# A two-model stack of ten phases: paired 512-column products and a hand-written order under the last blocks of each contraction

## The chip, the cores and the metric

The kernel runs on one core of a Trainium2 chip, as one launch. The metric is the device time of that core in microseconds, the median of several runs. The times before are 2337.38, 2338.28 and 2340.46 us (median 2338.28).

## The reference, cut to what matters

Two transformer stacks run one after the other on 256 tokens of width 1024 (`x`), the first with 256 context tokens (`ctx`) beside them. All tensors are fp32.

```python
def half_ffn(h, m, k, g_pre, g_post, w_in, w_out):          # first stack, D_FF = 2816
    y = swiglu(modulated_norm(h, g_pre, m, k), w_in, w_out)
    return gated_residual(h, y, g_post, m, k, 0.5)
# layer 0: half_ffn (x and ctx), differential attention, half_ffn (x and ctx)
# layer 1: half_ffn (x and ctx), grouped attention (x alone onward), half_ffn (x)
def gated_residual(h, y, g, m, k, weight):
    return h + weight * m[..., k + 2, :] * rmsnorm(y, g)
# second stack, one layer
x = x + 0.5 * swiglu_2(rmsnorm_2(x, norm_ffn1), ffn1_gate, ffn1_up, ffn1_down)
x = x + merged(dilated attention, block attention, two gates) @ w_out
x = x + 0.5 * swiglu_2(rmsnorm_2(x, norm_ffn2), ffn2_gate, ffn2_up, ffn2_down)
return rmsnorm_2(x, norm_final)
```

So there are nine contractions back to width 1024 (six SwiGLU, two attention outputs, the mixer's output), and each is followed by a residual, a norm over the row, and the next phase's products.

## The kernel before, in words

**Numbers.** Every fp32 operand is split into a high part (rounded to fp32r) and a low part (the rest). A product is three matmuls into one PSUM tile (`mm3`, L126 to L130): high by high (L128), weights high by low or low by high (L129), and the third cross term (L130). A weight is loaded by DMA into `raw`, split by ScalarE (high, L118) and VectorE (low, L119) into `wh`, `wl` (or into arena units `u`).

**Phases.** `run` goes through ten phases: three SwiGLU phases on 512 tokens (`T == 512`), differential attention (512 tokens, after the first of them), grouped attention, three SwiGLU phases on 256 tokens (`T == S`), the hybrid mixer (256 tokens, before the last of these), and a final norm. Within a SwiGLU phase the features go by pairs of 128-blocks: `half(q, c, t0, t1)` (L668) multiplies one 128-block of the gate (`q = 0`) or up (`q = 1`) weights with the input over 8 blocks of 128 rows; that is 24 matmuls of 256 columns on 256 tokens and 24 of 512 columns on 512 tokens. `post` (L677) takes SiLU of the gate PSUM tile, multiplies with the up tile and splits the result. On 256 tokens the first two of the eleven pairs are done token by token (`lead_tokens`, L624), the other nine by `half`. In the mixer, `project` (L1310) does 8 blocks by `columns` (L552), also 24 matmuls of 256 columns. In differential attention, six of the eight heads are projected in between the attention steps: `first` does the first 256 tokens of a block, `second` the other 256.

**The end of a contraction (an edge).** `contract` (L414) runs over the rows of the down weight. The last 4 or 6 row blocks (the tail) go token tile by token tile, so that tile 0 is done first, then its residual and norm can run while the PE works on tile 1. `gated` (L358) is the residual of the first stack: `products` multiplies with the gate row (VectorE, L368) and then squares the same half for the norm (ScalarE, L340); `stat` takes the root on GpSimd (L346); `add` adds into `h` (L378). `stats` (L486) of the next phase squares `h` (L340), takes the root, scales the rows (L502); `turn` (L506) transposes them on the PE (L514) and applies scale and bias: ScalarE into a scratch tile (L523), VectorE copy to the high part (L524) and difference to the low (L525), or without bias L123 and L124. Then the first products of the next phase (its leads) can start. `Order` collects all these steps with due times worked out from the length of the pieces and calls them in that order. The framework's scheduler then orders the emitted instructions of each engine by its own model, so that the due times set priorities and not the final order.

**Queues.** SyncE issues nearly all DMAs; `raw` has 5 buffers, `wh`/`wl` share 8, scratch tiles have 6, PSUM 8 banks. ScalarE, VectorE and GpSimd each run their instructions in the order in which they stand.

## Time and profile before

| | before |
|---|---|
| median of 3 runs | 2338.28 us |
| the profiled execution | 2339.77 us |
| its span (first to last instruction) | 2338.0 us |
| PE busy | 2277.9 us, 97% |
| DVE busy | 1471.0 us, 63% |
| ACT busy | 1016.7 us, 43% |
| matmuls | 13275 |

PE is the matmul engine, DVE is VectorE, ACT is ScalarE, POOL is GpSimd. The ends of matmuls in the trace are modelled and overlap, so a matmul's cost is read from start to start (its pitch), and a short PE stall shows as a longer pitch, not as idle time. Nine edges stand in the trace; eight lie at 380, 680, 1040, 1418, 1532, 1724, 1920 and 2120 us (30 us each), the ninth at the end. They are called edges 1 to 9 below. Edges 1 to 4 lead into phases on 512 tokens, edges 5 to 8 into phases on 256; from edge 6 on the rows of the next phase need no bias. A view by windows gives, for each stretch, its length, then the busy time of PE, PEld (weight loads), DVE, ACT and POOL with the count of instructions, the granted PE clock, the DMA share and GB/s.

### The profile page before, as it was taken

Reading aid. Unit: us, or ns where it says so; the run is one execution under the profiler, and the core shown is the slowest. Engines: PE = TensorE matmul, PEld = TensorE weight load, DVE = VectorE, ACT = ScalarE, POOL = GpSimd, SP = SyncE. Lnnn points to the kernel's source line nnn. Section 1 sums busy time; section 2 is a strip of 40 time slices with the busy share of each in tenths; the row PEclk is TensorE's granted clock in tenths of the full one; section 3 lists DMA queues with packets and bytes.
Section 4 is the critical chain, followed back from the end, with each engine's and each line's share of the span. In section 5 each row is a group of like instructions: output and inputs, shape, how many; then the busy total and the mean of one; then the engine's idle time right before and its main releaser. Section 6 shows DMA issues by size and latency. Waiting matters only on the chain.

```text
span 2338.0 us, 33744 instructions
## 1 busy us (share of the span) xinstructions
PE 2277.9 (97%) x13275; PEld 1984.2 (85%) x13275; DVE 1471.0 (63%) x2334; ACT 1016.7 (43%) x1831; POOL 84.7 (4%) x130
## 2 busy tenths in 40 slices
PE   7999999998899999999999999999999999999998
PEld 5888887888788788888888887789989989999997
DVE  4866474578767753746866626775555557877554
ACT  4322223566653232134322225765445546655543
POOL 0000000111100000000000001100000002000000
PEclk9999999999999999999999999999999999999999
DMA  9655364321225643652665542145665575546664
GB/s 283 210 186 180 117 228 133 100 64 38 90 72 163 181 146 106 218 160 73 203 185 170 168 139 78 55 154 181 191 197 162 181 235 169 144 129 198 172 181 143
DMA packets 270951, 361.46 MB, mean 155 GB/s; under 512 B 11472, under 2 KB 222280, under 8 KB 270792
## 3 DMA queue, kind: packets, MB, share of 16 engines
q1 hardware_dynamic: 270464, 359.17, 49.5%
q8 instruction: 104, 1.70, 0.3%
q14 instruction: 55, 0.45, 0.1%
q10 hardware_dynamic: 328, 0.14, 0.0%
HBM read 355.02 MB, written 4.24 MB: 154 GB/s over the span
## 4 chain that ended last, share of the span: by engine, by line
PE 60%; DVE 5%; ACT 3%; issue 1%; DMA 1%; POOL 1%; POOLq 0%; DVEq 0%; ACTq 0%
PE ps L128 19%; PE ps L129 19%; PE ps L130 19%; DVE u L119 1%; DVE wl L119 1%; ACT junk L340 1%; DVE u L378 1%; ACT u L118 0%; DVE s_l L525 0%; ACT wh L118 0%; PE ps L514 0%; POOL sm L346 0%; DVE scr L368 0%; PE ps L257 0%; DMA raw<-in_ffn_up_dram 0%
## 5 line engine op out<-in xcount | busy, mean ns | idle before, releaser
L128 PE MATMUL ps<-s_h,wh 128*128 128x256 f32 (+1 forms) x2560 | 835.3, 327 | 5.5 <-ACT u L1019 3.6
L129 PE MATMUL ps<-s_l,wh 128*128 128x256 f32 (+1 forms) x2560 | 831.7, 325 | 0.6 <-DVE s_l L525 0.5
L130 PE MATMUL ps<-s_h,wl 128*128 128x256 f32 (+1 forms) x2560 | 830.2, 324 | 0.2 <-DVE wl L119 0.2
L119 DVE TENSOR_TENSOR wl<-raw,wh 128x1024 fp32r<-128x1024 f32 x458 | 550.3, 1210 | 422.3 <-ACT wh L118 420.6
L118 ACT ACTIVATE wh<-raw 128x1024 fp32r<-128x1024 f32 x458 | 475.1, 1047 | 572.8 <-PE ps L129 509.9
L128 PEld LDWEIGHTS ps<-s_h,wh 128*128 128x128 f32 x2560 | 486.6, 190 | 52.0 <-ACT u L1019 4.2
L129 PEld LDWEIGHTS ps<-s_l,wh 128*128 128x128 f32 x2560 | 486.8, 190 | 41.7 <-DVE s_l L525 2.3
L130 PEld LDWEIGHTS ps<-s_h,wl 128*128 128x128 f32 x2560 | 486.7, 190 | 39.4 <-DVE wl L119 0.4
L128 PE MATMUL ps<-wh,s_h 128*128 128x512 f32 (+1 forms) x976 | 367.0, 376 | 0.4 <-DVE s_h L524 0.4
L129 PE MATMUL ps<-wl,s_h 128*128 128x512 f32 (+1 forms) x976 | 363.8, 373 | 0.0
L130 PE MATMUL ps<-wh,s_l 128*128 128x512 f32 (+1 forms) x976 | 363.5, 373 | 0.0
L244 DVE SCALAR_TENSOR_TENSOR u<-raw,sc,u 128x1024 f32<-128x1024 f32 x224 | 277.1, 1279 | 80.3 <-DMA raw<-in_ada_w_dram 80.1
L128 PEld LDWEIGHTS ps<-wh,s_h 128*128 128x128 f32 x976 | 184.5, 189 | 33.0 <-DVE s_h L524 0.6
L130 PEld LDWEIGHTS ps<-wh,s_l 128*128 128x128 f32 x976 | 184.2, 189 | 32.2
L129 PEld LDWEIGHTS ps<-wl,s_h 128*128 128x128 f32 x976 | 184.4, 189 | 31.1
L118 ACT ACTIVATE s_h<-scr 128x256 fp32r<-128x256 f32 (+1 forms) x144 | 74.1, 514 | 304.2 <-DVE scr L682 287.1
L129 PE MATMUL ps<-u,s_h 128*128 128x512 f32 (+1 forms) x312 | 117.2, 376 | 1.3 <-DVE u L119 1.3
L128 PE MATMUL ps<-u,s_h 128*128 128x512 f32 (+1 forms) x312 | 117.8, 378 | 0.0
L130 PE MATMUL ps<-u,s_l 128*128 128x512 f32 (+1 forms) x312 | 116.9, 375 | 0.0
L682 DVE TENSOR_TENSOR scr<-scr,ps 128x512 f32<-128x512 f32 (+1 forms) x120 | 67.6, 564 | 77.6 <-PE ps L130 75.9
L680 ACT ACTIVATE scr<-ps 128x512 f32<-128x512 f32 (+1 forms) x120 | 58.8, 493 | 106.2 <-PE ps L130 99.5
L346 POOL TENSOR_TENSOR sm<-sm,mhalf 128x1 f32<-128x1 f32 x50 | 27.5, 553 | 1993.8 <-DVE sm L345 1993.8
(183 smaller groups left out, 1941.0 us busy)
## 6 DMA issues: line engine op xcount, KB each, us to landing
raw<-in_ffn_w_in_dram SPq DMA_DIRECT2D x176, 512.0 KB, 4.1
raw<-in_ada_w_dram SPq DMA_DIRECT2D x144, 512.0 KB, 4.6
raw<-in_ffn_w_out_dram SPq DMA_DIRECT2D x88, 512.0 KB, 4.1
raw<-in_ffn_gate_dram SPq DMA_DIRECT2D x44, 512.0 KB, 5.3
raw<-in_ffn_up_dram SPq DMA_DIRECT2D x44, 512.0 KB, 5.0
raw<-in_ffn_down_dram SPq DMA_DIRECT2D x44, 512.0 KB, 4.3
raw<-in_w_in_dram SPq DMA_DIRECT2D x44, 512.0 KB, 4.8
raw<-in_da_w_in_dram SPq DMA_DIRECT2D x24, 512.0 KB, 3.8
```

Source lines behind the costliest of these rows:

```text
L118: self.nc.scalar.activation(hi, src, AF.Copy)
L119: self.nc.vector.tensor_tensor(lo, src, hi.bitcast(F32), ALU.subtract)
L128: mm(out, lhi, rhi, start=start, stop=False)
L129: mm(out, lhi, rlo, start=False, stop=False)
L130: mm(out, llo, rhi, start=False, stop=stop)
L244: nc.vector.scalar_tensor_tensor(acc[s][h], raw, x, acc[s][h], ALU.mult, ALU.add)
L340: self.nc.scalar.activation(self.junk, src, AF.Square, scale=1.0 / 32, accum_out=ss)
L346: nc.gpsimd.tensor_tensor(r, v, self.mhalf, ALU.pow)
L378: nc.vector.scalar_tensor_tensor(h[:, sl], st.yg[k], st.r, h[:, sl], ALU.mult, ALU.add)
L680: self.nc.scalar.activation(sg, pg[:, 0:T], AF.Silu)
L682: self.nc.vector.tensor_tensor(hf, sg, pu[:, 0:T], ALU.mult)
```

## The change

1. **Paired parts.** A new class `Pair` keeps the high and the low part of one input block side by side in 512 columns. `mm_pair` multiplies the weights' high part with both at once (one matmul of 512 columns in place of two of 256), leaving the two sums in the two halves of the PSUM tile, and the weights' low part with the high part (256 columns). `halves` adds them: a ScalarE copy of the right half and a VectorE add of the left. It is used in `half` on 256 tokens and in the mixer's `project`. The low-part matmuls stand last but one.
2. **Row-block pieces.** In differential attention `first` and `second` each do 4 row blocks over all 512 columns, in place of 8 row blocks over 256 columns each.
3. **Gate first.** SiLU is taken right after the gate's product, ahead of the up product.
4. **Squares ahead.** In `gated` the squares of a half are a step of their own, ahead of the gate products of the same half, and `stat` comes ahead of the second products.
5. **Written order.** All that `Order` issues at an edge is put in a region in which every engine keeps the written order. The due times are new (a 512-column matmul 0.227 instead of 0.216), transposes of the first two tiles are spread by 1.8 us, those of the other two stand after all four leads, and the leads' weights are loaded from 0.5 or 1 us on after the tail's beginning.
6. **Bias.** In `turn`, every second block's high part is written by ScalarE straight from PSUM, not by a VectorE copy.

```diff
+class Pair:
+    def __init__(self, pool, name, nblk):
+        self.u = [pool.tile([P, 2, 512], F32R, tag="u", name=f"{name}_p{u}") for u in range(nblk // 2)]
+    def both(self, k):
+        return self.u[k // 2][:, k % 2, :]
+    def at(self, which, k, c0=0, c1=S):
+        return self.both(k)[:, S * which + c0:S * which + c1]
...
+    def mm_pair(self, out, w, x, n):
+        mm = self.nc.tensor.matmul
+        for b in range(n - 1):
+            mm(out, w(b)[0], x.both(b), start=b == 0, stop=False)
+        for b in range(n):
+            mm(out[:, 0:S], w(b)[1], x.at(0, b), start=False, stop=False)
+        mm(out, w(n - 1)[0], x.both(n - 1), start=False, stop=True)
...
+    def halves(self, p):
+        f = self.scr([P, S])
+        self.nc.scalar.activation(f, p[:, S:512], AF.Copy)
+        self.nc.vector.tensor_tensor(f, f, p[:, 0:S], ALU.add)
+        return f
...
-        def products(k):
+        def squares(k):
             if k == 0:
                 st.ss = self.small(2)
+            self.half_squares(y[k], st.ss[:, k:k + 1])
+        def products(k):
             t = self.scr([P, 512])
             nc.vector.tensor_tensor(t, y[k], g[:, k * 512:(k + 1) * 512], ALU.mult)
-            self.half_squares(y[k], st.ss[:, k:k + 1])
             st.yg.append(t)
...
-        return [(-half, lambda: products(0)), (0.0, lambda: products(1)), (1.6, stat), (2.6, add)], 3.61, 0.6
+        return [(1.6 - half, lambda: squares(0)), (3.3 - half, lambda: products(0)), (0.0, lambda: squares(1)),
+                (0.9, stat), (1.0, lambda: products(1)), (1.9, add)], 3.4, 0.7
...
-        step = 0.216 * 6 * tail
+        step = 0.227 * 6 * tail
...
-        o.issue()
+        with self.tc.manual_schedule():
+            o.issue()
...
-        return [(-half, lambda: squares(0)), (0.0, lambda: squares(1)), (1.0, rstd), (1.8, rows)], 1.85
+        return [(-half, lambda: squares(0)), (0.0, lambda: squares(1)), (0.9, rstd), (1.8, rows)], 2.8
...
+                if q % 2:
+                    modulate(hi)
+                else:
+                    nc.vector.tensor_copy(hi, f)
...
-        self.xT = self.k.asplit(KB, self.T)
+        self.xT = k.asplit(KB, self.T) if self.T == 512 else Pair(k.ar, k.nm("s"), KB)
...
-                    o.add(ready[2 * s + 1] + (1.76, 0.0)[s] + 0.33 * kk,
+                    o.add((ready[1] + 1.8 * kk, self.go + 8.8 + 0.01 * kk)[s],
...
-            o.add(t_end - 5.86 + q, lambda q=q: dma(q))
-            o.add(t_end - 5.66 + 4 * q, lambda q=q: split(q))
+            o.add(0.5 + q, lambda q=q: dma(q))
+            o.add(1.5 + 2.5 * q, lambda q=q: split(q))
...
+        if self.T == S:
+            self.k.mm_pair(p, w, self.xT, KB)
+            return
...
+    def gate_values(self, pg):
         k, T = self.k, self.T
+        x = k.halves(pg) if T == S else pg
+        sg = x if T == S else k.scr([P, T])
+        self.nc.scalar.activation(sg, x, AF.Silu)
+        return sg
+    def post(self, j, sg, pu):
+        k, T = self.k, self.T
+        if T == S:
+            pu = k.halves(pu)
...
-                    self.columns(r.p, r.w, 0, S)
+                    self.columns(r.p, r.w, 0, 512, range(4))
...
-                    self.columns(r.p, r.w, S, 512)
+                    self.columns(r.p, r.w, 0, 512, range(4, KB))
...
-        self.columns(p, self.k.wcols(self.w, c0), 0, S)
-        return p[:, 0:S]
+        k.mm_pair(p, lambda b: [x[:, b, :] for x in w], self.xT, KB)
+        return k.halves(p)
```

**Place A**, the PE in a SwiGLU phase on 256 tokens: `s..h` and `s..l` are input blocks (high, low), `wh` and `wl` weights, a name's number a buffer. Before, six matmuls of one half:

```order
L128 MATMUL ps2772_15697<-s2664_h0_15004,wh2767_15688 128x256
L129 MATMUL ps2772_15697<-s2664_l0_15005,wh2767_15688 128x256
L130 MATMUL ps2772_15697<-s2664_h0_15004,wl2768_15689 128x256
L128 MATMUL ps2772_15697<-s2664_h1_15006,wh2769_15692 128x256
L129 MATMUL ps2772_15697<-s2664_l1_15007,wh2769_15692 128x256
L130 MATMUL ps2772_15697<-s2664_h1_15006,wl2770_15693 128x256
```

Now a whole half, 16 matmuls:

```order
L151 MATMUL ps2449_13317<-s2332_p0_12674,wh2445_13309 128x512 x2
L151 MATMUL ps2449_13317<-s2332_p1_12675,wh2445_13309 128x512 x2
L151 MATMUL ps2449_13317<-s2332_p2_12676,wh2447_13313 128x512 x2
L151 MATMUL ps2449_13317<-s2332_p3_12677,wh2447_13313 128x512
L153 MATMUL ps2449_13317<-s2332_p0_12674,wl2446_13310 128x256 x2
L153 MATMUL ps2449_13317<-s2332_p1_12675,wl2446_13310 128x256 x2
L153 MATMUL ps2449_13317<-s2332_p2_12676,wl2448_13314 128x256 x2
L153 MATMUL ps2449_13317<-s2332_p3_12677,wl2448_13314 128x256 x2
L154 MATMUL ps2449_13317<-s2332_p3_12677,wh2447_13313 128x512
```

The L128 and L129 of a block have become one row of 512 columns, and the low weights come after seven of the eight wide ones.

**Place B**, ScalarE at edge 6: `wh`, `u` from `raw` are weight splits of the next phase's leads, `junk` from `ps` the squares of the contraction's halves (`ps2600`, `ps2601` tile 0), `junk` from `u` the squares of the next norm, `s` from `ps` the transposed rows. Before:

```order
L118 ACTIVATE u2679_15054<-raw2677_15044 128x1024
L340 ACTIVATE junk_80,sm2683_15068<-ps2600_14688 128x512
L118 ACTIVATE u2681_15058<-raw2678_15046 128x1024
L340 ACTIVATE junk_80,sm2683_15068<-ps2601_14689 128x512
L340 ACTIVATE junk_80,sm2688_15111<-u1147_6110 128x512 x2
L340 ACTIVATE junk_80,sm2689_15120<-ps2602_14702 128x512
L123 ACTIVATE s2664_h0_15004<-ps2694_15137,n2c_595 128x128 x3
L123 ACTIVATE s2664_h1_15006<-ps2695_15156,n2c_595 128x128
```

Now (`ps2618`, `ps2619` are tile 0):

```order
L132 ACTIVATE u2697_14585<-raw2695_14581 128x1024
L132 ACTIVATE u2699_14589<-raw2696_14583 128x1024
L371 ACTIVATE junk_80,sm2701_14605<-ps2618_14217 128x512
L371 ACTIVATE junk_80,sm2701_14605<-ps2619_14218 128x512
L371 ACTIVATE junk_80,sm2706_14642<-u1147_5825 128x512 x2
L371 ACTIVATE junk_80,sm2710_14664<-ps2620_14231 128x512
L137 ACTIVATE s2682_p0_14533<-ps2711_14666,n2c_595 128x128 x2
L137 ACTIVATE s2682_p1_14534<-ps2711_14666,n2c_595 128x128 x2
L137 ACTIVATE s2682_p2_14535<-ps2712_14685,n2c_595 128x128 x2
```

Both lead splits now stand ahead of both squares, and the transposed blocks of one PSUM tile are done in a row, not mixed with the other's.

**Place C**, VectorE at the same edge: L368 is now L402 (gate products), L345 is L376 (sum for the root), L378 is L411 (add). Before:

```order
L368 TENSOR_TENSOR scr2684_15069<-ps2600_14688,u2593_14674 128x512
L119 TENSOR_TENSOR u2680_15055<-raw2677_15044,u2679_15054 128x1024
L119 TENSOR_TENSOR u2682_15059<-raw2678_15046,u2681_15058 128x1024
L368 TENSOR_TENSOR scr2685_15090<-ps2601_14689,u2593_14674 128x512
L345 SCALAR_TENSOR_TENSOR sm2686_15099<-sm2683_15068 128x1
```

Now:

```order
L133 TENSOR_TENSOR u2698_14586<-raw2695_14581,u2697_14585 128x1024
L133 TENSOR_TENSOR u2700_14590<-raw2696_14583,u2699_14589 128x1024
L402 TENSOR_TENSOR scr2702_14613<-ps2618_14217,u2611_14203 128x512
L376 SCALAR_TENSOR_TENSOR sm2703_14622<-sm2701_14605 128x1
L402 TENSOR_TENSOR scr2705_14626<-ps2619_14218,u2611_14203 128x512
```

The second products have gone behind the sum for the root, and no weight split stands between the two halves of tile 0. On the PE at edge 1 the first eight transposes stood after 84 of the tail's 96 matmuls; now the first four stand after 78, four more after 90, and the other eight at the end.

## Rows read from the trace of the kernel before

**Rows 1.** The page: busy us, share of the span and instructions per engine.

```profile
PE 2277.9 (97%) x13275; PEld 1984.2 (85%) x13275; DVE 1471.0 (63%) x2334; ACT 1016.7 (43%) x1831; POOL 84.7 (4%) x130
```

**Rows 2.** Timeline, 256-column matmuls (start us, us, engine, line, operation, out<-in).

```profile
1800.10 0.28 PE L128 MATMUL ps<-s_h,wh 128*128 128x256 f32 x1
...
1804.78 0.28 PE L128 MATMUL ps<-s_h,wh 128*128 128x256 f32 x1
```

**Rows 3.** Timeline, 512-column matmuls.

```profile
299.84 0.39 PE L130 MATMUL ps<-wh,s_l 128*128 128x512 f32 x1
...
303.92 0.39 PE L130 MATMUL ps<-wh,s_l 128*128 128x512 f32 x1
```

**Rows 4.** Timeline, 128x256 operations like those that halves adds.

```profile
1800.84 0.36 ACT L680 ACTIVATE scr<-ps 128x256 f32<-128x256 f32 x1
...
1802.82 0.42 DVE L682 TENSOR_TENSOR scr<-scr,ps 128x256 f32<-128x256 f32 x1 [0.63 <-PE ps L130]
```

**Rows 5.** Windows of three stages and of the half-clock stretches.

```profile
480.00:660.00 180.00, 163.34 (x1138) 148.14 (x1138) 139.65 (x406) 113.90 (x304) 27.83 (x40) 0.96 0.17 57
619.00:626.00 7.00, 5.61 (x23) 4.91 (x24) 5.52 (x20) 4.41 (x13) 0.73 (x1) 0.52 0.84 285
640.00:646.00 6.00, 6.00 (x22) 5.24 (x23) 4.00 (x17) 2.56 (x9) 0.69 (x1) 0.50 0.00 0
1742.00:1746.00 4.00, 4.00 (x17) 3.32 (x16) 1.70 (x5) 1.22 (x4) 0.00 (x0) 0.57 0.00 0
1760.00:1920.00 160.00, 160.00 (x1159) 152.19 (x1158) 89.23 (x104) 79.41 (x104) 0.00 (x0) 1.00 0.63 195
1945.00:2010.00 65.00, 62.48 (x505) 60.98 (x504) 53.30 (x111) 49.05 (x110) 8.01 (x9) 1.00 0.56 159
```

**Rows 6.** Windows of edges 1 to 8, 30 us each: the sum.

```profile
sum 240.00, PE 228.15 PEld 194.26 DVE 156.70 ACT 130.61 POOL 32.85; mean PE 28.52 PEld 24.28 DVE 19.59 ACT 16.33 POOL 4.11
```

**Rows 7.** Timeline of the PE at edge 6: tail's first matmul, then the transposes.

```profile
1724.80 0.39 PE L128 MATMUL ps<-u,s_h 128*128 128x512 f32 x1
...
1739.53 0.39 PE L130 MATMUL ps<-u,s_l 128*128 128x512 f32 x1
1741.78 0.74 PE L514 MATMUL ps<-ident,u 128*128 128x128 f32 x4 [1.86 <-DVE u L502]
```

**Rows 8.** Timeline of ACT at edge 6: lead split, squares, transposed blocks.

```profile
1731.16 1.06 ACT L118 ACTIVATE u<-raw 128x1024 fp32r<-128x1024 f32 x1 [0.27 <-DMA raw<-in_ffn_gate_dram]
...
1733.38 1.05 ACT L118 ACTIVATE u<-raw 128x1024 fp32r<-128x1024 f32 x1
1736.38 0.60 ACT L340 ACTIVATE junk<-ps 128x512 bf16<-128x512 f32 x1 [1.96 <-DVE scr L368]
...
1742.55 0.37 ACT L123 ACTIVATE s_h<-ps,n2c 128x128 fp32r<-128x128 f32 x1 [0.66 <-PE ps L514]
1743.33 0.37 ACT L123 ACTIVATE s_h<-ps,n2c 128x128 fp32r<-128x128 f32 x1 [0.42 <-DVE s_l L124]
```

**Rows 9.** Timeline of DVE at edge 6: lead split, products, rows.

```profile
1735.61 0.68 DVE L368 TENSOR_TENSOR scr<-ps,u 128x512 f32<-128x512 f32 x1
...
1741.23 0.88 DVE L502 TENSOR_SCALAR u<-u,sm 128x512 f32<-128x512 f32 x2
```

**Rows 10.** Timeline of ACT at edge 1: tile 1's norm squares, first scaled blocks.

```profile
398.07 0.63 ACT L340 ACTIVATE junk<-u 128x512 bf16<-128x512 f32 x1
...
401.53 1.93 ACT L523 ACTIVATE scr<-ps,mods,amod 128x256 f32<-128x256 f32 x4 [1.26 <-PE ps L514]
```

**Rows 11.** Timeline of the PE at edge 1: tail's first matmul, transposes, first lead.

```profile
380.31 0.39 PE L128 MATMUL ps<-u,s_h 128*128 128x512 f32 x1
...
400.95 0.98 PE L514 MATMUL ps<-ident,u 128*128 128x128 f32 x7 [1.32 <-DVE u L502]
...
406.83 0.28 PE L128 MATMUL ps<-s_h,wh 128*128 128x256 f32 x1
...
409.43 0.28 PE L128 MATMUL ps<-s_h,wh 128*128 128x256 f32 x1
```

More of the change, by code (lines that the diff above doesn't have):

```diff
@@ L522, in turn @@
                 f = k.scr([P, w])
-                nc.scalar.activation(f, pt[:, q, :], AF.Identity, scale=A[:, b:b + 1], bias=B[:, b:b + 1])
-                nc.vector.tensor_copy(hi, f)
+                modulate = lambda to: nc.scalar.activation(to, pt[:, q, :], AF.Identity,
+                                                           scale=A[:, b:b + 1], bias=B[:, b:b + 1])
+                modulate(f)
+                if q % 2:
+                    modulate(hi)
+                else:
+                    nc.vector.tensor_copy(hi, f)
                 nc.vector.tensor_tensor(lo, f, hi.bitcast(F32), ALU.subtract)
     def enter(self, o, done, t_end):
-        self.xT = self.k.asplit(KB, self.T)
+        k = self.k
+        self.xT = k.asplit(KB, self.T) if self.T == 512 else Pair(k.ar, k.nm("s"), KB)
         self.xn = [None] * self.nt
@@ L534, in enter @@
             ready.append(done[t][0] + took)
-        self.go = max(t_end, ready[self.nt // 2 - 1] + (1.76 + 3 * 0.33 + 0.1 if self.T == 512 else 0.97 + .1))
+        self.go = max(t_end, ready[self.nt // 2 - 1] + (5.5 if self.T == 512 else 1.1))
         self.ready = ready
@@ L545, in enter @@
                 for kk in range(2):
-                    o.add(ready[t] + 0.97 * kk, lambda t=t, kk=kk: self.turn((t,), range(4 * kk, 4 * kk + 4)))
+                    o.add(ready[t] + 1.0 * kk, lambda t=t, kk=kk: self.turn((t,), range(4 * kk, 4 * kk + 4)))
         self.lead(o, t_end)
@@ L550, in lead, with columns @@
         pass
-    def columns(self, p, w, t0, t1):
+    def columns(self, p, w, t0, t1, blocks=range(KB)):
         hi, lo = w
-        for b in range(KB):
+        for b in blocks:
             self.k.mm3(p[:, t0:t1], hi[:, b, :], lo[:, b, :],
@@ L618, in lead @@
         for q in range(2):
-            o.add(t_end - 5.86 + q, lambda q=q: dma(q))
-            o.add(t_end - 5.66 + 4 * q, lambda q=q: split(q))
+            o.add(0.5 + q, lambda q=q: dma(q))
+            o.add(1.5 + 2.5 * q, lambda q=q: split(q))
             for c in range(2):
-                o.add(self.go + 5.2 * q + 2.6 * c, lambda q=q, c=c: self.half(q, c, 0, S))
+                o.add(self.go + 5.8 * q + 2.9 * c, lambda q=q, c=c: self.half(q, c, 0, S))
     def lead_tokens(self, o, t_end):
@@ L670, in half @@
         p = self.p[q][c]
[L671 to L680 removed]
+        cc = slice(c * P, (c + 1) * P)
+        w = lambda b: [x[:, b % 4, cc] for x in self.w[q][b // 4]]
+        if self.T == S:
+            self.k.mm_pair(p, w, self.xT, KB)
+            return
+        for b in range(KB):
+            self.k.mm3(p[:, t0:t1], *w(b), self.xT.at(0, b, t0, t1), self.xT.at(1, b, t0, t1), b == 0, b == KB - 1)
+    def gate_values(self, pg):
+        k, T = self.k, self.T
+        x = k.halves(pg) if T == S else pg
[6 more added lines that the diff above has]
+            pu = k.halves(pu)
         hf = k.scr([P, T])
[L682 removed]
+        self.nc.vector.tensor_tensor(hf, sg, pu, ALU.mult)
         k.split(self.hT.at(0, j), self.hT.at(1, j), hf)
@@ L707, in body @@
             t0 = self.begun if jp == 0 else 0
+            pg = [None, None]
             for q in range(2):
@@ L716, in body @@
                         late.pop(0)()
-                    if q:
+                    if q == 0:
+                        pg[c] = self.gate_values(p[c])
+                    else:
                         self.post(2 * jp + c, pg[c], p[c])
-                pg = p
                 if jp + 1 < NJ // 2:
@@ L879, in lead @@
             self.started.append(r)
-            o.add(t_end - 8 + 2.6 * n, lambda r=r, h=h, part=part: self.block(part, h, r))
-            o.add(self.go + 2.6 * n, lambda r=r: self.columns(r.p, r.w, 0, S))
+            o.add(1 + 1.3 * n, lambda r=r, h=h, part=part: self.block(part, h, r))
+            o.add(self.go + 2.9 * n, lambda r=r: self.columns(r.p, r.w, 0, S))
     def setup(self, o, t_end):
@@ L1121, in load @@
                 self.wq[kp] = k.wpair(self.w, kp, 0)
-            o.add(t_end - 8 + 2.6 * kp, load)
-            o.add(self.go + 2.6 * kp, lambda kp=kp: piece(kp))
+            o.add(1 + 1.3 * kp, load)
+            o.add(self.go + 2.9 * kp, lambda kp=kp: piece(kp))
     def rope_tables(self, o, t_end):
@@ L1310, in project @@
     def project(self, c0):
-        p = self.k.ps()
-        self.columns(p, self.k.wcols(self.w, c0), 0, S)
-        return p[:, 0:S]
+        k = self.k
+        p = k.ps()
+        w = k.wcols(self.w, c0)
+        k.mm_pair(p, lambda b: [x[:, b, :] for x in w], self.xT, KB)
+        return k.halves(p)
     def lead(self, o, t_end):
```

8 lines of the change are left out of this document (removed).

## The prediction, made before the changed kernel was run

> **What bounds the kernel now.** The page comes first: the PE is busy for 97% of the span, VectorE for 63%, ScalarE for 43% [rows 1]. So time goes only where the PE does less or waits less. Next the pitch of its matmuls: from 1800.10 to 1804.78 us lie 39 starts of 256 columns, 0.1200 us each [rows 2]; from 299.84 to 303.92 lie 18 starts of 512 columns, 0.2267 us each [rows 3]. Twice the columns cost 1.89 times the pitch, so a matmul has a part that does not grow with its columns: 2 x 0.1200 - 0.2267 = 0.0133 us. Last, the windows of edges 1 to 8: of 240 us the PE was busy for 228.15, so 11.85 us of idle time lie there [rows 6], and in differential attention (480 to 660 us) another 16.7 us [rows 5]. The clock is full but for a few stretches: 7 and 6 us around 619 and 640 us, 4 us at 1742 us stand at half or nearly half [rows 5], each right behind a lull of the PE (at 1742 the wait of 1.86 us [rows 7]).
>
> **Pairing in the SwiGLU phases.** Three phases x 9 pairs x 4 halves = 108 halves, each with 8 high-part pairs: 864 times two matmuls of 256 columns become one of 512. Saved: 864 x 0.0133 = 11.5 us, all on the engine that bounds. Added: 144 times (108 here, 36 in the mixer) a ScalarE copy of 0.36 and a VectorE add of 0.42 us [rows 4], 52 and 60 us in all. Here they lie beside the PE: in 1760 to 1920 us VectorE is busy for 89.23 of 160 us and ScalarE for 79.41 [rows 5]; four adds and copies per pair of about 11 us bring them to some 71% and 63%. Were that cover gone, a pair could lose up to 4 x 0.42 us, which I exclude at these shares. The gate's PSUM tiles come free earlier than before; the low weights are needed 1.6 us later within a half. I take -11.5 us.
>
> Here a page speaks against the change. The rows say 0.0133 us for one matmul fewer [rows 2, 3]. The Trainium skill, "TensorE: Matmul & The Clock Gate", section "Wait — 56ns, not 53.3ns?", puts the cost of a matmul beyond its columns at about 2.5 ns. By the page, 1440 merges (864 + 288 + 288) would give 3.6 us in place of 19.2 by the rows. The trace disagrees with it for this kernel's pairs of weight load and matmul, and the sum goes by the rows.
>
> **Pairing in the mixer.** 36 projections x 8 = 288 merges, -3.8 us at most. From 1945 to 2010 us VectorE is already busy for 53.30 of 65 us and ScalarE for 49.05 [rows 5]; the 17 projections begun there add 17 x 0.42 = 7.1 and 17 x 0.36 = 6.1, so 93% and 85%. That fits, but rows of a softmax will queue behind the adds. Against it, the later splits read a copy in SBUF, so the two engines need not take turns on one PSUM bank. Bounds: -3.8 (all covered) and +4 (a quarter of the 15.1 us of adds of all 36 projections comes out); I take -0.8, nearer the cover, since 93% is still below the limit.
>
> **Row-block pieces.** 12 blocks x 24 = 288 merges, -3.8 us. But from 480 to 660 us the PE already idles 16.7 us, with VectorE busy for 139.65 of 180 [rows 5]: part of the gain becomes waiting. Bounds -3.8 and 0; I take half, -1.9.
>
> **The edges.** At edge 6 the tail begins at 1724.80, so tile 0 ends 36 pitches on, at 1732.96 [rows 3, 7]. Yet its second gate product started at 1735.61 [rows 9], because VectorE had a lead's weight split in front, whose ScalarE half ran only from 1733.38, behind the first squares; the second squares followed at 1736.38, since they wait for the product on the same PSUM tile [rows 8]. From these squares to the end of the rows (1741.23 + 0.88 = 1742.11 [rows 9]) it takes 5.73 us. The PE had nothing from 1739.76 and waited 1.86 us [rows 7], and the clock then fell to half for 3.4 us, 1.7 us lost [rows 5]. In the new order both splits end by about 1733.2, the two squares by 1734.6, so the second begins near 1733.9 and the rows end at 1739.6: the wait goes. What is late next is the turn: ScalarE and VectorE alternate on one PSUM tile, one block per 0.78 us (1742.55 to 1743.33 [rows 8]), and the new order does all of one tile first, where the old one mixed two. The first block is taken up 0.77 us after the first transpose (1741.78 to 1742.55), so the last of 8 is ready 0.77 + 8 x 0.78 = 7.0 us after it; the first lead starts 1.8 us of due time and four more transposes (0.74 [rows 7]) after it and wants the last block 21 pitches of 0.1200 later, 5.0 us in all, so up to 2.0 us come back. Edge 6: between -3.6 and 0, I take -1.6.
>
> At edges 1 to 3 the rows of tile 1 come late for another reason: its norm squares started at 398.07 [rows 10], although tile 1 had left the PE at 391.2 (48 pitches after the tail's first matmul at 380.31 [rows 11]): ScalarE stood at squares of tile 2. The PE waited 1.32 us, and its first lead then ran at a stretched pitch: 9 pitches from 406.83 to 409.43 took 2.60 in place of 1.08 us [rows 11], waiting for scaled blocks. Now the chain of a tile stands unbroken; at 5.7 us it ends at 397.1, and the first transposes stand after 78 tail matmuls, at 398.0. So 1.3 + 1.5 us per edge are to be had. Against it, ScalarE gets three operations per two blocks in place of two, four of which take 1.93 us [rows 10], about 0.45 each: 1.35 us per two blocks, so the last blocks of the first lead come some 1 us late, and for the second two tiles, whose transposes now stand behind all leads, 4 x 1.35 = 5.4 us run against 5.8 us of products. I take -1.5 for each. Edge 4 has no such products right behind: -2.0. Edges 5, 7 and 8 lost little: -0.5 together. The sum is -8.6; as several moves are untried in one written order, I take -7.
>
> Its bounds: -13.6 (all 11.85 idle us and 1.7 of clock), and +5 (no wait goes, edge 6 gets 2.0 and four edges 0.8 each). The new waits sit on ScalarE: leads' splits stand ahead of the squares, and should their DMA land late, the squares, the root, the rows and then the PE all wait behind them.
>
> **Gate first, bias, the end.** Moving SiLU changes no count; the third ScalarE operation of a pair is in the edges' term; the last chain after edge 9 keeps its operations. Zero, covered by the PE.
>
> **Sum.** -11.5 - 0.8 - 1.9 - 7 = -21.2 us. Against the profiled execution (2339.77, span 2338.0) that is 2318.6; it lies 1.5 above the median of the runs, so the median becomes 2338.28 - 21.2 = 2317.
>
> **Rivals.**
> 1. *The waits move.* The edges and both mixers give nothing: 2338.3 - 11.5 = 2327. For it: each edge has a second wait close behind the first. Against it: the 1.3 to 1.9 us waits have plain causes that the order removes.
> 2. *The fixed part stays.* What a matmul costs beyond its columns belongs to the operands, not to the count, and a wide pair keeps it but for the 2.5 ns: 3.6 + 7 = 10.6, 2328. This is the page's rule named above; the measured pitches speak against it.
> 3. *More comes out.* All idle time of the edges goes with its clock (13.6), pairing in both mixers holds 2.7, and one of the half-clock stretches in differential attention (7 us, 3.5 lost) does not come up: 11.5 + 13.6 + 2.7 + 3.5 = 31, 2307.
> 4. *Slower: head-of-line waits.* With every engine bound to the written order, a lead's split on ScalarE waits for its DMA in front of the squares at each edge. Pairing gives 14.2; from 14.2 / 8 = 1.8 us per edge more than now it is lost. At 3 us per edge, half a microsecond above the second lead split's lateness at edge 6 (it starts at 1733.38 [rows 8], 0.4 after tile 0's end) plus two splits of 1.06: 2338.3 - 14.2 + 24 = 2348. At 1.8: no change.
>
> **How the numbers follow.** Chances: forecast 0.51 (2312 to 2322), rival 1 0.22 (2322 to 2333), rival 2 0.04, rival 3 0.15 (2302 to 2312), no change (rival 4 at its turning point) 0.03, rival 4 0.05. A difference of 0.2%, 4.7 us, is about what a measurement of this kernel can tell from no change; faster by more 0.92, within 0.03, slower 0.05. The range holds the forecast, the upper part of rival 3 and most of rivals 1 and 2: 2306 to 2329.
>
> **What would show it.** In the trace after: 512-column matmuls at 0.227 us in the SwiGLU phases on 256 tokens and about 11.1 us per pair with the PE always busy (pairing right); the window sum of the edges with under 7 us idle, and no half clock behind edge 6 (edges right); VectorE above 90% in the mixer with PE waits for softmax rows (rival 1 there). Wrong would be: a pitch of 0.24 in the pairs, ScalarE idle for a DMA just ahead of the squares, or new half-clock stretches.

## The result, and the profile of the changed kernel

The changed kernel takes 2358.66 us (median of 5 runs, 2348.69 to 2359.95) beside 2337.38 us before: a ratio of 1.0076 with a 95% interval of 1.0059 to 1.0092, that is 14 to 22 us slower. The forecast was 2317. Two of its runs lie near 2349 (granted clock 0.994 over the run) and three near 2359 (0.99); the profiled execution is one of the former, 2349.54 us with a span of 2347.8.

The page, engines, answers to [rows 1]: 1440 matmuls fewer, and yet the PE is busy for only 2.3 us less.

```profile
PE 2275.6 (97%) x11835; PEld 1910.5 (81%) x11835; DVE 1520.8 (65%) x2438; ACT 1080.7 (46%) x2015; POOL 81.9 (3%) x130
```

One `half` in a SwiGLU phase on 256 tokens, PE, answers to [rows 2, 3] (a row holds several matmuls):

```profile
1802.15 1.77 PE L151 MATMUL ps<-s_p,wh 128*128 128x512 f32 x7
1803.76 1.12 PE L153 MATMUL ps<-s_p,wl 128*128 128x256 f32 x8
1804.71 0.40 PE L154 MATMUL ps<-s_p,wh 128*128 128x512 f32 x1
1804.95 1.77 PE L151 MATMUL ps<-s_p,wh 128*128 128x512 f32 x7
```

From 1802.15 to 1804.95 a half takes 2.80 us; 24 matmuls of 0.1200 took 2.88. The pairing does what it says. The windows of the edges answer to [rows 5, 6] (edge 6, edge 8, sum of all eight):

```profile
1724.00:1754.00 30.00, 29.93 (x168) 25.35 (x167) 18.48 (x33) 15.27 (x34) 2.20 (x4) 1.00 0.48 154
...
2120.00:2150.00 30.00, 25.00 (x102) 19.76 (x101) 21.65 (x33) 17.06 (x26) 0.55 (x1) 0.89 0.67 215
sum 240.00, PE 225.97 PEld 189.81 DVE 156.51 ACT 143.64 POOL 32.41; mean PE 28.25 PEld 23.73 DVE 19.56 ACT 17.95 POOL 4.05
```

The eight edges together hold 14.0 us of idle time, 11.85 before; the forecast had under 7. Edge 6 lost its wait and its half clock, as forecast. Edge 8, where little was lost before, now holds 5 us of idle time and a clock of 0.89. There VectorE shows the cause:

```profile
2134.24 1.23 DVE L133 TENSOR_TENSOR wl<-raw,wh 128x1024 fp32r<-128x1024 f32 x1 [0.57 <-ACT wh L132]
2135.73 1.23 DVE L133 TENSOR_TENSOR wl<-raw,wh 128x1024 fp32r<-128x1024 f32 x1 [0.27 <-ACT wh L132]
2137.14 1.22 DVE L133 TENSOR_TENSOR u<-raw,u 128x1024 fp32r<-128x1024 f32 x1 [0.18 <-ACT u L132]
2138.71 1.23 DVE L133 TENSOR_TENSOR u<-raw,u 128x1024 fp32r<-128x1024 f32 x1 [0.34 <-ACT u L132]
2139.85 1.28 DVE L419 SCALAR_TENSOR_TENSOR u<-ps,u 128x512 f32<-128x512 f32 x2
```

The tail began at 2125.48, and this is the last of tile 0's 36 matmuls:

```profile
2134.17 0.39 PE L144 MATMUL ps<-u,s_l 128*128 128x512 f32 x1
```

The tile's residual (L419) started at 2139.85, 5.3 us after that matmul's end: in the written order six weight splits of the next phase stand ahead of it (two more ahead of the four shown, from 2130.88 on). These wait for ScalarE's half of the split, and ScalarE waits for the weights:

```profile
2136.05 1.06 ACT L132 ACTIVATE u<-raw 128x1024 fp32r<-128x1024 f32 x1 [0.35 <-DMA raw<-in_ffn_gate_dram]
2137.62 1.06 ACT L132 ACTIVATE u<-raw 128x1024 fp32r<-128x1024 f32 x1 [0.50 <-DMA raw<-in_ffn_gate_dram]
```

The PE, same place, waits 4.80 us and then runs at a pitch of 0.42 in place of 0.23; the granted clock of the window from 2144 to 2148 us is 0.50, that is 1.2 GHz:

```profile
2143.45 1.12 PE L549 MATMUL ps<-ident,u 128*128 128x128 f32 x4 [4.80 <-DVE u L537]
...
2144.79 0.63 PE L143 MATMUL ps<-u,s_h 128*128 128x512 f32 x1
2145.21 0.63 PE L144 MATMUL ps<-u,s_l 128*128 128x512 f32 x1
```

The sharpest view is the time from one tail's first matmul (L128 or L142 with `ps<-u,s_h`, 512 columns) to the next one's, since a shift at one edge then stays in its row. From the profiled executions, in us (the last four columns are experiments told of below; a row is named by the edge that it starts with and the phase behind it):

| stretch | before | after | a_free | b_edges | b_edges_free | a_free_unpair |
|---|---|---|---|---|---|---|
| start to edge 1 | 380.31 | 381.44 | 381.95 | 380.94 | 380.65 | 380.30 |
| edge 1, differential attention | 285.19 | 282.35 | 280.01 | 287.09 | 280.04 | 279.94 |
| edge 2, SwiGLU 512 | 372.91 | 373.10 | 370.28 | 373.06 | 370.29 | 370.30 |
| edge 3, SwiGLU 512 | 374.93 | 375.64 | 372.98 | 375.66 | 372.99 | 372.95 |
| edge 4, grouped attention | 120.49 | 122.10 | 119.95 | 121.99 | 120.00 | 120.00 |
| edge 5, SwiGLU 256 | 190.97 | 189.87 | 187.80 | 192.54 | 190.58 | 188.34 |
| edge 6, SwiGLU 256 | 193.37 | 191.03 | 186.75 | 194.09 | 189.82 | 186.74 |
| edge 7, mixer | 205.88 | 209.95 | 211.44 | 206.74 | 207.76 | 207.80 |
| edge 8, SwiGLU 256 | 190.67 | 199.03 | 189.27 | 204.87 | 191.16 | 191.31 |
| edge 9 to the end | 23.26 | 23.25 | 23.26 | 23.25 | 23.25 | 23.26 |

Kernels with the same code in a row differ by up to 4.6 us in the first two rows (last section), and by up to 1.4, 2.4 and 3.5 in the rows of edges 2, 4 and 8. The other rows repeat within 0.6, those of edges 3, 6 and 7 within 0.1.

### The profile page after: what moved, and what is told of

Same layout as the page of the kernel before. It is cut to its first block, busy times and chain, and to the rows that moved or that the text cites. A ratio compares the mean times of both kernels' runs of the same rounds, so it can differ in the third digit from the quotient of the medians.

```text
span 2347.8 us, 31169 instructions
## 1 busy us (share of the span) xinstructions
PE 2275.6 (97%) x11835; PEld 1910.5 (81%) x11835; DVE 1520.8 (65%) x2438; ACT 1080.7 (46%) x2015; POOL 81.9 (3%) x130
## 4 chain that ended last, share of the span: by engine, by line
PE 63%; DVE 3%; ACT 3%; DMA 1%; issue 1%; POOL 0%; POOLq 0%; DVEq 0%; ACTq 0%
PE ps L142 15%; PE ps L144 15%; PE ps L143 15%; PE ps L151 9%; PE ps L153 6%; PE ps L154 1%; DVE wl L133 1%; PE ps L549 1%; DVE u L133 1%; DMA raw<-in_ffn_w_in_dram 0%; DMA raw<-in_ffn_gate_dram 0%; PE ps L288 0%; ACT wh L132 0%; ACT junk L371 0%; ACT u L132 0%
## 5 line engine op out<-in xcount | busy, mean ns | idle before, releaser
L142 PE MATMUL ps<-s_h,wh 128*128 128x512 f32 (+1 forms) x1312 | 489.9, 376 | 11.6 <-DVE s_h L564 5.5
L143 PE MATMUL ps<-s_l,wh 128*128 128x512 f32 (+1 forms) x1312 | 488.9, 373 | 0.5
L144 PE MATMUL ps<-s_h,wl 128*128 128x512 f32 (+1 forms) x1312 | 487.2, 372 | 0.0
L142 PE MATMUL ps<-wh,s_h 128*128 128x512 f32 x784 | 308.1, 393 | 0.0
L143 PE MATMUL ps<-wl,s_h 128*128 128x512 f32 x784 | 306.2, 391 | 0.0
L144 PE MATMUL ps<-wh,s_l 128*128 128x512 f32 x784 | 305.8, 390 | 0.0
L142 PEld LDWEIGHTS ps<-s_h,wh 128*128 128x128 f32 x1312 | 246.5, 189 | 61.9 <-DVE s_h L564 6.7
L143 PEld LDWEIGHTS ps<-s_l,wh 128*128 128x128 f32 x1312 | 246.9, 188 | 44.7 <-DVE s_l L565 2.8
L144 PEld LDWEIGHTS ps<-s_h,wl 128*128 128x128 f32 x1312 | 246.8, 188 | 42.5
L151 PE MATMUL ps<-s_p,wh 128*128 128x512 f32 x1008 | 258.2, 395 | 1.4 <-DVE scr L160 1.4
L151 PEld LDWEIGHTS ps<-s_p,wh 128*128 128x128 f32 x1008 | 187.9, 189 | 37.4 <-DVE scr L160 1.3
L142 PEld LDWEIGHTS ps<-wh,s_h 128*128 128x128 f32 x784 | 148.0, 189 | 30.3 <-DVE scr L1124 0.2
L142 PE MATMUL ps<-u,s_h 128*128 128x512 f32 x264 | 104.9, 398 | 0.4 <-ACT u L132 0.4
```

The costliest lines, as they stand in the source:

```text
L142: mm(out, lhi, rhi, start=start, stop=False)
L143: mm(out, lhi, rlo, start=False, stop=False)
L144: mm(out, llo, rhi, start=False, stop=stop)
L151: mm(out, w(b)[0], x.both(b), start=b == 0, stop=False)
```

## Experiments: the written order

**a_free**, the change without its region:

```diff
-        with self.tc.manual_schedule():
-            o.issue()
+        o.issue()
```

> The changed kernel without the region in which every engine keeps the written order; the due times and all else stay as changed, the scheduler orders the engines again. Theory O (the order costs the time): the eight edges, which together lost 16 us of PE time against before, come back to about where they were, edge 8 above all (its 4.8 us wait and the half clock behind it go), and the time is about 2333 us, faster than before. Theory T (the weights of the leads come late at edge 8 because of the transfers themselves, whatever the order): edge 8 still waits and the time stays above 2345 us.

Measured: 2328.36 us, ratio to before 0.9964 (0.9951 to 0.9977). Taking the region away turns 0.8% slower into 0.4% faster; every edge but edge 7 gets back 2 to 10 us (the 2.2 of edge 4 lie within what its row varies by). Of the 9.8 us at edge 8, the wait of 4.80 stands against 1.91 in a_free, and some 3.3 us (30 x 0.11) went to the clock. Theory O holds, theory T falls.

**b_manual**, the kernel before with the region alone:

```diff
-        o.issue()
+        with self.tc.manual_schedule():
+            o.issue()
```

> The kernel before with one change: what is issued at an edge stands in the region in which every engine keeps the written order; the due times are the old ones. Theory O (a written order binds every engine to due times that know nothing of when weights land): slower than before, by 10 us or more. Rival D (only the new due times are bad, a written order as such is harmless): within 4 us of before.

Measured: 2378.69 us, 1.0174 (1.0155 to 1.0193), 42 us slower than before by medians. Its longest group of PE waits (engine, line, releaser: us in total, times, longest):

```profile
PE ps L515 <- DVE u L503: 29.6, 13, 5.6
```

13 times the PE waits for the scaled rows, the last link of a tile's chain. So it is not the new due times: a written order by the old ones is worse still.

**b_edges** and **b_edges_free**, the kernel before with parts 4, 5 and 6 of the change (squares ahead, due times, turn), with the region and without; pairing and row-block pieces are left away.

> The kernel before with all that the change does at the edges (squares ahead, due times, turn, region), without pairing and without row-block pieces. Theory O: 10 to 20 us above before, 2348 to 2358. If the loss needs pairing at the edges (its narrower pairs, its copies and adds): about 2338 or less.

Measured: 2361.74 us, 1.0099 (1.0079 to 1.0119), 25 us slower than before by medians, more than the 10 to 20 expected.

> The same without the region: squares ahead, new due times and the new turn, but the scheduler orders the engines. Theory O: the moves themselves are worth what the sum of the prediction gave them, about 7 to 9 us, so 2329 to 2331. If the moves are worth nothing or harm: 2338 or more.

Measured: 2332.04 us, 0.9976 (0.9964 to 0.9989); 4.7 us less than before by medians, somewhat under the 7 to 9 expected, and the interval holds 3 to 8. So the moves are worth most of what they promised, in the scheduler's hands; the region alone costs the difference of the two, 30 us.

**f_reg8**, the best kernel (a_free_unpair, below) with the region at edge 8 alone:

```diff
-        o.issue()
+        if getattr(nxt, 'n', 0) == 2:
+            with self.tc.manual_schedule():
+                o.issue()
+        else:
+            o.issue()
```

> The best kernel so far with the region of the written order at edge 8 alone. Theory O: at edge 8 the adds of tile 0 stand on VectorE behind six weight splits that wait for their weights, the PE waits about 5 us and then runs at half clock; 8 to 12 us slower than without, 2331 to 2335 us, all of it in the 48 us behind the tail's start. If the loss at edge 8 needs the pairing in the mixer or the written order of the edges ahead of it: under 3 us.

Measured: 2336.02 us, 0.9991 (0.9982 to 1.0), 13 us above a_free_unpair by medians, a little more than the 8 to 12 expected; in the profiles the stretch behind edge 8 takes 201.50 in place of 191.31, 10.2 us, and no stretch ahead of it changes by as much as 2 us. The PE's waits for scaled rows:

```profile
PE ps L552 <- DVE u L540: 5.8, 2, 4.9
```

Nearly the same wait (4.9 us) as in the changed kernel (4.80), with the mixer unpaired and no other edge written out. One edge in a written order is enough.

**a_late8**, the changed kernel with two of the three lead splits of edge 8 put later in the written order:

```diff
-            o.add(t_end - 18.63 + 1 + 2.57 * n, lambda jp=jp, q=q: split(jp, q))
+            o.add((-1.3, 11.2, 13.5)[n] if getattr(self, 'n', 0) == 2 else t_end - 17.63 + 2.57 * n, lambda jp=jp, q=q: split(jp, q))
```

> The changed kernel, written order kept; at edge 8 alone the second and third of the three lead weight splits are issued behind the rows of tile 0 (due 11.2 and 13.5 us instead of 1.3 and 3.8). Theory O: VectorE no longer stands at a split whose weights have not landed while the residual of tile 0 is ready, the 4.8 us wait of the PE goes and with it the half clock; 8 to 11 us less than the changed kernel, 2338 to 2341 us beside its 2349. Theory T: under 3 us less.

Measured: 2352.13 us, 1.0067 (1.0052 to 1.0083), no gain that can be told from the changed kernel; the stretch behind edge 8 takes 197.43 in place of 199.03. VectorE there (the tail began at 2134.53; the last matmul of tile 0 ended at 2143.67, that of tile 1 at 2152.80):

```profile
2143.41 1.28 DVE L419 SCALAR_TENSOR_TENSOR u<-ps,u 128x512 f32<-128x512 f32 x2
...
2156.73 2.36 DVE L133 TENSOR_TENSOR u<-raw,u 128x1024 fp32r<-128x1024 f32 x2 [1.21 <-ACT u L132]
2159.00 0.68 DVE L419 SCALAR_TENSOR_TENSOR u<-ps,u 128x512 f32<-128x512 f32 x1
```

and the PE:

```profile
2161.90 1.33 PE L549 MATMUL ps<-ident,u 128*128 128x128 f32 x5 [3.08 <-DVE u L537]
```

The residual of tile 0 is on time, and the wait of 4.8 is gone; but now the third split stands ahead of the second half of tile 1's residual (2159.00), and the PE waits 3.08 us for tile 1's rows. The expected number was missed, because in a written order a late split has to stand ahead of something.

Edges 1 to 3 show another cost of the written order, smaller, on ScalarE and without a DMA: squares that are due earlier stand ahead of blocks that the PE wants. Edge 2 in the changed kernel (tail from 663.79; L558 are transposed blocks of the first lead, L371 squares of later tiles):

```profile
685.33 1.02 ACT L558 ACTIVATE scr<-ps,mods,amod 128x256 f32<-128x256 f32 x2 [1.74 <-PE ps L549]
686.24 0.56 ACT L558 ACTIVATE s_h<-ps,mods,amod 128x256 fp32r<-128x256 f32 x1
686.69 0.63 ACT L371 ACTIVATE junk<-u 128x512 bf16<-128x512 f32 x1
...
687.44 0.63 ACT L371 ACTIVATE junk<-u 128x512 bf16<-128x512 f32 x1
...
688.20 0.60 ACT L371 ACTIVATE junk<-ps 128x512 bf16<-128x512 f32 x1
...
688.79 1.01 ACT L558 ACTIVATE scr<-ps,mods,amod 128x256 f32<-128x256 f32 x2
```

and its PE, which stands twice for those blocks:

```profile
689.72 0.39 PE L142 MATMUL ps<-s_h,wh 128*128 128x256 f32 x1 [0.73 <-DVE s_h L564]
692.36 0.38 PE L142 MATMUL ps<-s_h,wh 128*128 128x256 f32 x1 [1.09 <-DVE s_h L564]
```

In a_free (tail from 661.96; its line numbers are lower by one) the scheduler puts one square between two groups of blocks, and the PE has no such wait:

```profile
683.87 1.00 ACT L557 ACTIVATE scr<-ps,mods,amod 128x256 f32<-128x256 f32 x2
684.76 0.56 ACT L557 ACTIVATE s_h<-ps,mods,amod 128x256 fp32r<-128x256 f32 x1
685.21 0.60 ACT L371 ACTIVATE junk<-ps 128x512 bf16<-128x512 f32 x1
...
685.78 1.03 ACT L557 ACTIVATE scr<-ps,mods,amod 128x256 f32<-128x256 f32 x2
```

At edge 6 the region costs 4.3 us (191.03 beside 186.75), though the first wait is gone: five starts of the leads come 0.28 us late there, at a rate of one block of the turn per 0.79 us (the prediction had feared this of the turn), and two more come 0.7 us late for weight splits. In a_free one start of the leads is late, by 0.22.

## Experiments: pairing and row-block pieces

**b_pair**, the kernel before with paired parts in the SwiGLU phases on 256 tokens alone (parts 1 and 3 of the change without the mixer), and **b_pair_rb**, the same with the row-block pieces (part 2).

> The kernel before with paired parts in the three SwiGLU phases on 256 tokens alone (mixer, edges, differential attention as before). If a merge of two 256-column matmuls saves 0.013 us and the added copies and adds lie beside the PE: 11.25 us less than before, about 2327. If the added work on ScalarE and VectorE shows: over 2333.

Measured: 2329.54 us, 0.9961 (0.9948 to 0.9975): 6 to 12 us less.

> As the run before it, with the row-block pieces of differential attention added. If the merges there come out of the PE's path: 3.7 us less again, about 2323. If they turn into waits for VectorE: about 2327, no less than without them.

Measured: 2329.76 us, 0.9963 (0.995 to 0.9975), no less than without the pieces. In differential attention the profile lost 8.5 us to a reduced clock here and 1.7 in b_pair, which hides whatever the merges save. So the opposite edit was made on a steadier kernel: **f_norb**, the best kernel with the pieces taken back.

```diff
-                    self.columns(r.p, r.w, 0, 512, range(4))
+                    self.columns(r.p, r.w, 0, S)
...
-                    self.columns(r.p, r.w, 0, 512, range(4, KB))
+                    self.columns(r.p, r.w, S, 512)
```

> The best kernel so far (no region, projections of the mixer unpaired: 2322.9 us) with differential attention as before: 256-column pieces in place of the row-block pieces. If the 288 merges come out of the PE's path: 3.7 us slower, 2326.6. If what they save is given back there as idle time or as half clock: within 1.5 us of 2322.9.

Measured: 2324.92 us, 0.9945 (0.9928 to 0.9961), beside 0.9931 (0.9915 to 0.9948) with them: the intervals overlap. In the profiles, with 5.1 us lost to the clock in both (length times one less the granted clock), differential attention takes 282.20 without the pieces and 279.94 with them. Less what the clock took, the row is 274.4 to 274.9 in all eight kernels here that have the pieces and no region ahead of it, and 277.1 in f_norb. The pieces save 2.3 us where the clock is alike, and nothing that the runs can tell.

## Experiments: the mixer

**a_free_unpair**, a_free with the projections as before:

```diff
-        k.mm_pair(p, lambda b: [x[:, b, :] for x in w], self.xT, KB)
-        return k.halves(p)
+        for b in range(KB):
+            k.mm3(p[:, 0:S], w[0][:, b, :], w[1][:, b, :], self.xT.at(0, b), self.xT.at(1, b), b == 0, b == KB - 1)
+        return p[:, 0:S]
```

> The changed kernel without the region and with the mixer's projections as before (24 matmuls of 256 columns, no copies and adds); pairing in the SwiGLU phases, row-block pieces and the new due times stay. If the adds of the paired projections hold up the softmax rows on VectorE: the mixer's phase goes from 211 us back to 206 and the time is about 2323. If the mixer's loss is the edge ahead of it: it stays at 210 and the time at 2328.

Measured: 2322.91 us (2322.49 to 2323.12), 0.9931 (0.9915 to 0.9948). It beats both kernels. The mixer takes 207.80 in place of 211.44: pairing costs 3.6 us there, of which 1.7 are lost in a stretch at half clock that a_free has and a_free_unpair hasn't; by medians the two kernels differ by 5.5 us. (Of the 1.9 us over before, b_edges_free has as much with the mixer untouched: edge 7 loses by the new due times.)

Is it VectorE's load? **m_dve**, **m_act** and **m_both** put the added operations behind each unpaired projection, singly and together:

```diff
-        return p[:, 0:S]
+        f = k.scr([P, S])
+        self.nc.scalar.activation(f, p[:, 0:S], AF.Copy)
+        self.nc.vector.tensor_tensor(f, f, p[:, 0:S], ALU.max)
+        return f
```

(This is m_both. m_act leaves out the maximum; m_dve has one VectorE copy, `tensor_copy(f, p[:, 0:S])`, in place of both operations.)

> The best kernel so far with one VectorE copy of 128x256 (PSUM to SBUF, about 0.4 us) put behind each of the 36 projections of the mixer; the matmuls stay unpaired. Theory V (adds on VectorE hold up the softmax rows): the mixer's phase gets 4 to 7 us longer than 207.8, that is the loss of the paired version without its saved matmuls; about 2328. If ScalarE's copies are to blame: under 2 us.

Measured: 2322.84 us, 0.9939 (0.9924 to 0.9953); the mixer takes 207.09.

> As the run before it, but the copy is ScalarE's. Theory V: the mixer's phase stays within 2 us of 207.8, about 2324. If ScalarE's copies (or the projections' longer way into SBUF) are to blame: 4 to 7 us longer.

Measured: 2324.17 us, 0.9942 (0.9923 to 0.996); the mixer takes 207.53. Each is free by itself: theory V falls, and ScalarE's copies alone are not it either.

> The best kernel so far (mixer's projections unpaired, 2322.9 us) with both added operations behind each of the 36 projections: ScalarE's copy, then VectorE's operation on the copy and the PSUM tile (a maximum of the two, same shape and operands as the add of the paired version), matmuls unpaired. Theory C (not the load but the chain: the projection passes ScalarE's queue and then VectorE's, and the softmax operations stand behind it in the same queues): the mixer's phase gets 4 to 8 us longer than 207.8, about 2328. Theory P (the paired matmuls themselves: the PE is ahead sooner and only waits more): within 2 us of 207.8.

Measured: 2331.59 us, 0.9968 (0.9958 to 0.9978); the mixer takes 214.85, 7.05 more than without, 1.7 of it at half clock. The windows over the first attention steps of a_free_unpair, m_dve and m_both, in this order, say that it isn't VectorE's load alone:

```profile
1928.00:1993.00 65.00, 62.21 (x504) 60.69 (x505) 53.16 (x113) 47.65 (x109) 5.46 (x7) 1.00 0.55 159
```
```profile
1934.00:1999.00 65.00, 62.19 (x506) 60.76 (x506) 59.40 (x133) 50.48 (x111) 5.67 (x7) 1.00 0.57 163
```
```profile
1934.00:1999.00 65.00, 59.89 (x473) 58.01 (x472) 54.73 (x121) 50.90 (x119) 5.88 (x7) 0.97 0.56 158
```

VectorE is busiest in m_dve (59.40 of 65 us), where the PE works for 62.19; in m_both it has less to do (54.73), and the PE only 59.89. The PE's waits for softmax rows between 1890 and 2120 us, here in a_free and in m_both, point to the chain; in a_free_unpair they are 1.9 us and in m_dve 0.3:

```profile
PE ps L1439 <- DVE u L1429: 5.0, 6, 3.8
```
```profile
PE ps L1443 <- DVE u L1433: 5.3, 3, 3.0
```

VectorE in a_free, ahead of the PE's longest wait there:

```profile
1961.06 0.42 DVE L160 TENSOR_TENSOR scr<-scr,ps 128x256 f32<-128x256 f32 x1
1961.40 0.41 DVE L1422 SCALAR_TENSOR_TENSOR u<-u,ps 128x256 f32<-128x256 f32 x1
...
1966.22 0.34 DVE L1429 TENSOR_SCALAR u<-u,sm 128x256 f32<-128x256 f32 x1
```

ScalarE and the PE of the same:

```profile
1960.06 0.42 ACT L1514 ACTIVATE u<-scr 64x256 fp32r<-64x256 f32 x1
1960.39 0.36 ACT L159 ACTIVATE scr<-ps 128x256 f32<-128x256 f32 x1
```
```profile
1956.61 0.28 PE L1421 MATMUL ps<-u,u 128*128 128x256 f32 x1
...
1966.62 0.69 PE L1439 MATMUL ps<-ident,u 128*128 128x128 f32 x2 [3.79 <-DVE u L1429]
```

The scores were there from 1956.61 + 0.28. Their first softmax operation (L1422) stands behind a projection's add (L160), that waits for the projection's copy (L159), and the copy stands in ScalarE's queue behind the splits of the projection before. So the softmax of a step ends (L1429) when two queues have taken turns, and the PE waits 3.79 us. One rival is left: an operation on each of the two engines at once, neither waiting for the other, was not run. So the hop is told apart from the joint load by this reading of the trace, not by an experiment.

**m_pairmm** is a_free without the copy and the add, so that the product of the weights' high part with the input's low part is left out; **f_gatepair** is a_free_unpair with the 16 gates paired (the unpaired lines follow for the rest):

```diff
-        return k.halves(p)
+        return p[:, 0:S]
```
```diff
+        if c0 >= 3840:
+            k.mm_pair(p, lambda b: [x[:, b, :] for x in w], self.xT, KB)
+            return k.halves(p)
```

> The kernel without the region, mixer's projections by paired matmuls, but the sum of the two halves is left out: the consumers read the left half of the PSUM tile alone, as if that were the projection (so a third of the product is missing from the output). Theory C: with no copy and no add the merges are pure gain, the mixer's phase is about 204 us, 2319 in all. Theory P: 207 to 211 us, since the softmax operations bound the steps of the attention and what the PE saves becomes waiting.

Measured: 2324.17 us, 0.9939 (0.9924 to 0.9953); the mixer takes 205.35, 2.45 less than unpaired, nearer to theory C's 204 than to theory P's 207 to 211. The merges do save time there, two thirds of the count's 3.8.

> The best kernel so far with paired parts for the 16 gate projections of the mixer alone (their consumer is one ScalarE operation), the 20 projections of queries and keys unpaired. Theory C with the cost in the queries and keys, whose splits are chained through both engines: 1 to 2 us less than 2322.9. Theory P: 0 to 3 us more.

Measured: 2325.21 us, 0.9944 (0.9929 to 0.9959); the mixer takes 208.76, 1.0 more than unpaired where the merges alone would have given 1.7 less. The time is what theory P had expected here (0 to 3 us more), not theory C's 1 to 2 less: the cost isn't only in queries and keys. Part of it is a wait that a_free has too and a_free_unpair hasn't: in the mixer's phase the PE waits 1.4 us (two times, 1.2 the longer) with a paired projection (L151) for an add (L160). The rest stays open. The books nearly close: chain 7.05, merges -2.45, together +4.6 against the 3.6 measured for both at once.

## Why the prediction was wrong

**The edges, the step that failed.** The term was -7 with bounds of -13.6 and +5. Measured by itself, moves and region together, it is +25 us by medians (b_edges; 18 to 28). The mechanisms of the moves came true in part: in b_edges_free, without the region, the stretches behind edges 2, 3 and 6 shrink by 2.6, 1.9 and 3.6 us (forecast 1.5, 1.5, 1.6), edge 4 by 0.5 (forecast 2.0), while edges 5, 7 and 8 together lose 2.0 (forecast a gain of 0.5); the whole is 4.7 us faster. What failed is the step that took the order for a list of moves, each to be priced where it pays, and gave the region itself no price but the 1.6 us from -8.6 to -7. It costs 26 us (1.0076 against 0.9964), and 30 without pairing. This could have been seen. By the due times the first half of tile 0's residual comes 4.28 us after the tail's beginning and the splits at -1.29, 1.28 and 3.85, so all of them stand ahead of it; and the trace of before shows VectorE at edge 8 (tail from 2124.05; L385 is the residual, L119 the splits), where the scheduler let both halves of the residual pass splits whose weights were late:

```profile
2130.51 0.69 DVE L385 SCALAR_TENSOR_TENSOR u<-ps,u 128x512 f32<-128x512 f32 x1
...
2134.08 0.68 DVE L385 SCALAR_TENSOR_TENSOR u<-ps,u 128x512 f32<-128x512 f32 x1
...
2137.29 1.23 DVE L119 TENSOR_TENSOR u<-raw,u 128x1024 fp32r<-128x1024 f32 x1 [0.19 <-ACT u L118]
```
 
The prediction looked at the order at edges 1 and 6, where the weights are nearly in time (ScalarE waited 0.27 us for them at edge 6 [rows 8]), and carried it to edge 8, which it priced with edges 5 and 7 at -0.5 for having lost little. Here a place that lost little (the PE was busy for 29.21 of 30 us) is where the fixed order lost most. Two signs of being wrong that the prediction named stand in the trace: ScalarE idle for a DMA (2136.05, 2137.62) ahead of tile 0's squares (from 2140.57 on), and a new stretch at half clock.

**Rival 4 is what happened**, at a chance of 0.05: a split that waits for its DMA, ahead of a tile's chain. Its place and price were off in detail. It is VectorE's residual more than ScalarE's squares, and not 3 us at each edge but 2 to 4 at six edges, none at edge 7 and 10 at edge 8; at edges 1 to 3 no DMA is in it. Its sum, 10 us slower, was too small beside the 14 to 22 measured. The range of a written order should have reached further up. In the Trainium skill, "PSUM — Partial Sum Buffer", section "Engine vs sequencer instructions", the queues of ScalarE, VectorE and GpSimd are called strictly first in, first out. The traces agree (L419 at 2139.85 behind six splits).

**Pairing in the SwiGLU phases: right mechanism, a third too large.** 108 halves at 2.88 - 2.80 = 0.08 us are 8.6 us, not 11.5; b_pair measured 6 to 12, and in its profile the stretches behind edges 5, 6 and 8 shrink by 10.3 us, 1.7 of it clock. A wide matmul in a pair takes 0.230 us (7 in 1.61) and not the 0.2267 of [rows 3]. The cover held: from 1760 to 1920 us the PE is busy throughout. Rival 2 goes by the about 2.5 ns that the Trainium skill, "TensorE: Matmul & The Clock Gate", section "Wait — 56ns, not 53.3ns?", puts on a matmul beyond its columns. By that figure the half would take an estimated 24 x 0.1200 - 8 x 0.0025 = 2.86 us; the row says 2.80, so the trace disagrees with the skill for these pairs.

**Pairing in the mixer: wrong cause and wrong sign.** The forecast was -0.8 with -3.8 and +4 as bounds; it is +3.6 by the profiles, just inside them, and +5.5 by the medians. The price was hung on VectorE's busy share, and that was the wrong view: VectorE busy for 91% is free (m_dve), 84% with both operations in a row costs 7 us (m_both).

**Row-block pieces: about right.** Forecast -1.9, measured -2.3 where the clock is alike.

**The sum as it came out**: -8.6 + 3.6 - 2.3 - 5 + 26 to 30 = 14 to 18, beside 14 to 22 measured. The first four terms make -12.3, where a_free, which has just these, measured 5.4 to 11.5 us less; with the mixer's 5.5 by medians they make -10.4.

## What to carry to other kernels

Before fixing an order by hand, list for every engine what stands behind each instruction that waits for a DMA; where the trace shows a scheduler letting something pass such an instruction, a fixed order can pay that lateness in full, even where little is lost today. Moves and order are separate edits: keep the moves as priorities and let the scheduler order, then fix only what a trace shows to be wrong. And before pricing an added operation by the busy share of the engine that runs it, look at the hops that it puts between queues on the way to a waiting engine: here one operation on either engine cost nothing, and two in a row 7 us.
